# A plain first gate/up pair, modulation bursts placed anew at the feed-forward starts, and four bursts moved into the third layer's attention

## The chip, the cores and the metric

The kernel runs on one core of one Trainium2 chip. The metric is the device time of one execution in microseconds (us). Engines are named as in the profile: PE is TensorE (PEld its weight loads), DVE VectorE, ACT ScalarE, POOL GpSimd, and SP SyncE, which issues nearly all DMAs.

## The reference

One inference step of a four-layer diffusion transformer. 640 tokens (512 latent, 128 prompt) of 1024 features run through four layers, each with another attention: neighbourhood, sliding window, multi-head latent with low-rank queries and keys (MLA), and grouped queries. The latent and the prompt tokens have a modulation of their own in each layer, computed from the two conditioning vectors.

```python
def adaln(cond, w_mod, b_mod):
    m = jax.nn.silu(cond) @ w_mod + b_mod
    return [t[:, None, :] for t in jnp.split(m, 6, axis=-1)]

def modulate(h, shift, scale):
    return h * (1 + scale) + shift

def swiglu(h, w_gate, w_up, w_down):
    return (jax.nn.silu(h @ w_gate) * (h @ w_up)) @ w_down
...
    for li in range(DEPTH):
        mp = adaln(c_ctx[None, :], w_mod[li], b_mod[li])
        ms = adaln(c, w_mod[li], b_mod[li])
        hp = modulate(rms_norm(xp, norm1_g[li]), mp[0], mp[1])
        hs = modulate(rms_norm(xs, norm1_g[li]), ms[0], ms[1])
        ...
        xp = xp + mp[2] * op
        xs = xs + ms[2] * os_
        xp = xp + mp[5] * swiglu(modulate(rms_norm(xp, norm2_g[li]), mp[3], mp[4]), ffn_w_gate[li], ffn_w_up[li], ffn_w_down[li])
        xs = xs + ms[5] * swiglu(modulate(rms_norm(xs, norm2_g[li]), ms[3], ms[4]), ffn_w_gate[li], ffn_w_up[li], ffn_w_down[li])
```

`w_mod` is 1024 x 6144 per layer, the feed-forward's hidden width 2816.

## The kernel before, in words

Everything is float32. A product is made of three matmuls: each operand is split into a high and a low part (`hh`/`hl` for activations, `whi`/`wlo` for weights), and high x high, high x low and low x high are summed in a bank of PSUM. Features lie on the partitions in eight blocks of 128, tokens along the free axis in two halves of 320 (latent 0 to 319; latent 320 to 511 with the prompt), so that a matmul is 128 x 128 by 128 x 320. The split of a weight is one copy on ACT and one subtraction on DVE or POOL (`two`, L315).

**The feed-forward part** (`rest`, L798) first finishes the attention's output projection (`halves_first`, L580): the last two feature blocks are done first for one half of the tokens, then for the other. After each block, `stat` (L483) squares and sums the new features, and a matmul with a matrix of ones (tile `consts`) gives the sums over features; the reciprocal root of them scales the activations. `make_b` (L628) then makes the activations' high and low parts. Gate and up are computed in pairs of matrices of 256 hidden columns, 11 pairs a layer. Each matrix goes by the Strassen-Winograd scheme (`gate_up`, L707): weights and activations are cut into 2 x 2 quadrants, four sums of weights S1 to S4 (`make_a`, L684) and four combinations of activations T1 to T4 (`make_b`) replace the eighth product of quadrants, so that a matrix has seven blocks of 12 matmuls (`block`, L699) in place of eight. The quadrants "11" and "21" of the activations are the first half's, "12" and "22" the second's; "12" is used in combinations only. Block results are summed on DVE into the tiles `sv` and `y`. The down projection follows after 4, 4 and 3 pairs.

**The bursts.** The next layer's modulation is computed beside the feed-forward's matmuls. `mod_part` (L416) issues 16 small matmuls at a time (L424): the conditioning vectors against 4 tiles `rawm` of 512 KB, half of the rows of 1024 columns of `w_mod`. This group is called a burst here; the profile counts it as 32 rows. Two bursts make 1024 columns; their results are turned by two small matmuls (`modev`). `mod_load` (L448) issues the next four loads behind each burst; there are four buffers of `rawm`, so a load can start only when the burst before it has read them. `fill` (L468) issues one more burst, `rest` calls it twice behind the output projection (`EDGE`, L821), then in equal steps between the matrices, and twice at the end. The generator's first `fill` is the load alone.

**The order of the work.** Each engine runs its queue in order. The order is fixed when the program is built: a scheduler gives each instruction a place by its priority (the program's order, with `high_priority` and `issue_after` to move some) and by its own estimate of when operands are ready. PE, DVE and SP can thus run what the program writes later. Weights of 256 KB (`raw`) and the bursts' loads share SP's queue.

**The third layer's attention** (`Mla.body`, L1482) makes the first two heads' operands in `first_group` (L1639): queries of head group 0 are normalized on DVE, transposed on PE (`trs`, L1009), copied to `qn`; the rotary parts go through `pe2` and are transposed too; then the keys (`ktok`). `products_q(1)`, the 30 matmuls for the queries of the second head group, is written behind them, but before the change it ran ahead of the transposes. Then `units` computes scores, softmax and values. All bursts for the fourth layer's modulation are in the third's feed-forward part.

Of the kernel before, what the change touches and what calls it, by code (L numbers as in the profile page):

```python
# [14 lines left out]
P = 128  # L15
D = 1024
ND = 8
# [245 lines left out]
class Net:  # L263
# [6 lines left out]
    def mm(self, out, lhsT, rhs, start, stop):  # L270
        return self.nc.tensor.matmul(out, lhsT=lhsT, rhs=rhs, start=start, stop=stop, skip_group_check=True)  # L271

# [195 lines left out]
    def fill(self, n):  # L468

        for _ in range(n):  # L470
            while self.filler:
                try:
# [3 lines left out]
                    self.filler.pop(0)  # L476

    def flush(self):
        while self.filler:
            self.fill(1)  # L480
# [144 lines left out]
    def make_b(self, pool, L, B, raws):  # L625
# [36 lines left out]
        for i in range(HALF):  # L662
            for d in (i, i + HALF):
                raw(d, hi)
                p, m = raws[d][:, NL:], more[:, d:d + 1]
                nc.scalar.activation(p, p, AF.Identity, bias=m)
            a, b, t = raws[i], raws[i + HALF], t3[i // 2][:, i % 2]
            self.sub(nc.vector, t, b[:, hi], a[:, hi])
            self.sub(nc.vector, a[:, hi], a[:, hi], a[:, lo])
            two("T1", i, hi, a[:, hi])  # L670
# [7 lines left out]
        for i in range(HALF):  # L678
            two("T4", ND + HALF + i, lo, raws[i + HALF][:, lo])
        for i in range(HALF):  # L680
            two("22", i + HALF, hi, raws[i + HALF][:, hi], shift[:, i + HALF, 0:1])
        yield
# [15 lines left out]
    def block(self, out, A, B, start, stop):  # L698

        h, l = self.two(A, self.nc.vector)  # L700
        for k, (xh, xl) in enumerate(B):
            c = slice(k * P, (k + 1) * P)
            self.mm(out, h[:, c], xh, start and k == 0, False)
            self.mm(out, h[:, c], xl, False, False)
            self.mm(out, l[:, c], xh, False, stop and k == len(B) - 1)

    def gate_up(self, fp, L, name, i, B, pair):  # L707
# [31 lines left out]
        yield  # L739
        if i == 0:  # L740
            self.block(d, A["S1"], B["T1"], True, True)
        self.block(b, A["S2"], B["T2"], True, True)
        add(v1, b, s1)
        if i:
            self.block(d, A["S1"], B["T1"], True, True)
        self.block(b, A["S3"], B["T3"], False, True)
# [7 lines left out]
        if up:  # L754
            for r in (1, 0):
                hi, lo = (fp.tile([P, T], F32R, tag="a", name=n, bufs=16) for n in ("ah", "al"))
                nc.scalar.copy(hi, pair[r])
                self.sub(nc.vector, lo, pair[r], hi.bitcast(F32))
                pair[r] = (hi, lo)
        yield  # L760
# [38 lines left out]
    def rest(self, L):  # L799

        nc, tc, a = self.nc, self.tc, self.a
        with tc.tile_pool(name=f"ffn{L}", bufs=1, reuse_waits="tile") as fp:
            self.slots(fp)
            todo = 0
            if L + 1 < self.depth:
                c0 = self.mod_done.get(L + 1, 0)
                todo = (6144 - c0) // (4 * MODW) * (ND // BURST) + 1 - 2 * EDGE
                self.filler = [self.mod_parts(L + 1, c0, 6144, fp)]
            B, raws = {}, {}
            B_steps = self.make_b(fp, L, B, raws)  # L810
# [5 lines left out]
            def first_half(d):  # L816
                with tc.issue_after(self.last.ins):
                    next(B_steps)
            self.halves_first(lambda d: self.weights((L, "wo", d), 1), self.o_act[4:], L, 2, LAST,
                              after_wo, first_half)  # L820
            self.fill(EDGE)  # L821
            done = 0
# [4 lines left out]
            def ahead(m):  # L827
                n, i = mats[m]
                gens[m] = self.gate_up(fp, L, n, i, B, pairs[i])
                next(gens[m])  # L830
            ahead(0)
            ahead(1)
            next(gens[0])
            next(gens[1])
            next(B_steps)
            for part, (i0, i1) in enumerate(PAIRS):
                if part:
                    ahead(2 * i0)
                for m in range(2 * i0, 2 * i1):
                    if m > 1:  # L840
                        next(gens[m])
                    next(gens[m])
                    if 0 < m < 2 * i1 - 1:
                        ahead(m + 1)
                    next(gens[m])
                    while done < todo * (m + 1) // len(mats):
                        self.fill(1)
                        done += 1
# [16 lines left out]
class Attn:  # L865
# [142 lines left out]
    def tr(self, out, in_):  # L1008
        self.nc.tensor.transpose(out, in_, self.net.ident)  # L1009

# [468 lines left out]
class Mla(Full):  # L1479
# [4 lines left out]
    def body(self):  # L1484
# [9 lines left out]
        with net.tc.tile_pool(name="heads", bufs=1, reuse_waits="tile") as self.ap:  # L1494
            self.Q, self.ktok = {}, {}
            self.now(self.products_q(0), self.products_k(0))
            for g in range(4):
# [8 lines left out]
            self.job(net.out_part(2, 0), 16, 10, 16)  # L1506
            self.first_group()
            self.units()
            self.now(self.acts(8))
# [130 lines left out]
    def first_group(self):  # L1640
# [10 lines left out]
        for e in range(2):  # L1651
            x = self.tile([P, T], "qn", 3, F32R)
            self.stack(x, 64 * e, tl, net.col("mla_qn"))
            self.hd[e] = [x, None, None]
        pe = q[:, :, 256:]
        self.times(pe, ss[:, 1], 4, 32)
        self.rope(pe, 4, 16, self.qtab)

        pe2 = self.tile([P, NTT, P], "pe2")
        for e in range(2):  # L1660
# [7 lines left out]
        for e in range(2):  # L1668
            z = self.tile([P, T], "qpe", 2, F32R)
            self.stack(z, 64 * e, tl)  # L1670
            self.hd[e][2] = z
        tk = self.trs(k, slice(0, P), 6)
        for e in range(2):
# [4 lines left out]
            nc.scalar.copy(y[o, 1], y[r, 1].bitcast(F32))  # L1678
            self.hd[e][1] = y
        self.now(self.products_q(1))  # L1680
        for t in range(6):
            self.times(k[:, t:t + 1, P:], sk[:, t:t + 1, 2:], 2, 64, nc.gpsimd)
# [72 lines left out]
```

## Time and profile before

| | |
|---|---|
| runs, us | 3213.5, 3220.17, 3220.33 (median 3220.17) |
| profiled execution, us | 3216.05 (span 3214.0) |
| PE busy | 3029.7 us (94%), 21901 instructions |
| DVE, ACT, POOL busy | 67%, 48%, 19% |
| first FFN, from the end of attention to the second layer | about 378 to 881 us |
| third layer's attention | about 1635 to 1957 us |
| third FFN | about 1957 to 2461 us |

A busy PE is not yet a PE at its peak: matmuls overlap, and one is counted with its whole duration (313 ns for 128 x 320) although the next begins earlier. What a stretch is worth is read from the spacing of the matmuls' starts, and from the chain of waits, which follows the work that ended last back to the beginning.

### The profile page before, as it was taken

What the parts mean: (1) busy time and instruction counts of PE and PEld (TensorE: products, weight loads), DVE (VectorE), ACT (ScalarE), POOL (GpSimd) and SP (SyncE); (2) the same over time, 40 slices, a digit from 0 to 9 for tenths busy, and PEclk for the clock granted to TensorE, in tenths of its full rate; (3) what the DMA queues carried; (4) which work ended last, traced back from release to release, by engine and by line L of the source; (5) the groups of instructions that cost most, each with busy time, mean ns of one, the idle gap of its engine ahead of it and who ended that gap; (6) DMA issues with size and microseconds to landing.
All of it is one profiled execution on the core that took longest, in us unless ns stands there. A gap on an engine that the chain in (4) does not pass through costs nothing.

```text
span 3214.0 us, 57273 instructions
## 1 busy us (share of the span) xinstructions
PE 3029.7 (94%) x21901; PEld 2841.6 (88%) x21901; DVE 2161.6 (67%) x4522; ACT 1528.5 (48%) x3264; POOL 607.1 (19%) x691
## 2 busy tenths in 40 slices
PE   7998989999999989999986899899999999899999
PEld 6997879999988779999985778899998878799999
DVE  5555587666586768585768766867575775875765
ACT  4555454333356755242446664434243576543432
POOL 2553200000044420000025542000001553100000
PEclk9998999999999999999998999999999999899999
DMA  8346563232433342222211224522233111132322
GB/s 265 97 123 208 176 224 102 70 92 94 147 102 128 112 155 76 83 83 76 87 53 37 63 75 143 170 89 80 83 132 118 52 32 32 53 99 70 96 66 86
DMA packets 159027, 331.41 MB, mean 103 GB/s; under 512 B 18592, under 2 KB 40480, under 8 KB 158752
## 3 DMA queue, kind: packets, MB, share of 16 engines
q1 hardware_dynamic: 155584, 323.46, 32.3%
q8 instruction: 173, 2.83, 0.4%
q10 hardware_dynamic: 3168, 4.28, 0.4%
q14 instruction: 102, 0.84, 0.1%
HBM read 303.86 MB, written 4.28 MB: 96 GB/s over the span
## 4 chain that ended last, share of the span: by engine, by line
PE 81%; DVE 8%; DMA 5%; ACT 3%; issue 1%; POOL 1%; SPq 0%; DVEq 0%; ACTq 0%; POOLq 0%
PE big L271 53%; PE sm L271 18%; PE S L271 6%; PE tp L1009 3%; DMA rawm<-in_wmod 3%; DMA k<-k 1%; PE tp L271 1%; DMA raw<-in_wall 1%; DVE st L1030 1%; ACT p L1031 1%; DVE x L603 1%; DVE wlo L319 1%; ACT pt L285 0%; DVE qs L958 0%; DVE hl L999 0%
## 5 line engine op out<-in xcount | busy, mean ns | idle before, releaser
L271 PE MATMUL big<-hh,whi 128*128 128x320 f32 x2720 | 825.4, 313 | 11.7 <-ACT hh L645 5.6
L271 PE MATMUL big<-hl,whi 128*128 128x320 f32 x2720 | 829.0, 311 | 6.3 <-DVE hl L649 3.6
L271 PE MATMUL big<-hh,wlo 128*128 128x320 f32 x2720 | 821.0, 310 | 0.0
L318 ACT CAST whi<-raw 128x512 fp32r<-128x512 f32 (+2 forms) x636 | 383.3, 607 | 709.2 <-PE big L271 554.0
L271 PEld LDWEIGHTS big<-hh,whi 128*128 128x128 f32 x2720 | 508.8, 190 | 25.8 <-ACT hh L645 7.8
L271 PEld LDWEIGHTS big<-hl,whi 128*128 128x128 f32 x2720 | 510.1, 189 | 12.0 <-DVE hl L649 6.2
L271 PEld LDWEIGHTS big<-hh,wlo 128*128 128x128 f32 x2720 | 508.2, 189 | 0.1
L319 POOL TENSOR_TENSOR wlo<-raw,whi 128x512 fp32r<-128x512 f32 (+2 forms) x148 | 196.7, 1342 | 1634.0 <-ACT whi L318 1600.6
L319 DVE TENSOR_TENSOR wlo<-raw,whi 128x512 fp32r<-128x512 f32 (+1 forms) x488 | 325.1, 670 | 142.1 <-ACT whi L318 136.1
L318 ACT CAST whi<-sum 128x512 fp32r<-128x512 f32 x352 | 217.6, 619 | 300.1 <-PE big L271 264.6
L271 PE MATMUL big<-ah,wlo 128*128 128x320 f32 x1408 | 329.1, 309 | 0.0
L271 PE MATMUL big<-ah,whi 128*128 128x320 f32 x1408 | 329.0, 310 | 0.0
L271 PE MATMUL big<-al,whi 128*128 128x320 f32 x1408 | 328.6, 309 | 0.0
L319 DVE TENSOR_TENSOR wlo<-sum,whi 128x512 fp32r<-128x512 f32 x352 | 240.8, 684 | 54.5 <-ACT whi L318 52.9
L1041 POOL TENSOR_SCALAR p<-p,st 128x640 f32<-128x640 f32 (+2 forms) x256 | 197.7, 778 | 285.2 <-DVE st L1040 172.0
L603 DVE SCALAR_TENSOR_TENSOR x<-big,mod,x 128x128 f32<-128x128 f32 (+2 forms) x384 | 146.2, 432 | 150.7 <-PE big L271 150.3
L271 PEld LDWEIGHTS big<-ah,whi 128*128 128x128 f32 x1408 | 237.3, 188 | 1.3 <-issue 0.8
L271 PEld LDWEIGHTS big<-al,whi 128*128 128x128 f32 x1408 | 237.3, 188 | 0.3
L271 PEld LDWEIGHTS big<-ah,wlo 128*128 128x128 f32 x1408 | 237.3, 188 | 0.2
L271 PE MATMUL sm<-whi,hh 128*128 128x256 f32 (+1 forms) x770 | 225.1, 297 | 1.7 <-DVE qs L287 1.1
L271 PE MATMUL sm<-wlo,hh 128*128 128x256 f32 (+1 forms) x770 | 223.3, 292 | 0.2 <-POOL wlo L319 0.2
L271 PE MATMUL sm<-whi,hl 128*128 128x256 f32 (+1 forms) x770 | 223.1, 291 | 0.0
(260 smaller groups left out, 5419.3 us busy)
## 6 DMA issues: line engine op xcount, KB each, us to landing
raw<-in_wall SPq DMA_DIRECT2D x676, 256.0 KB, 2.6
rawm<-in_wmod SPq DMA_DIRECT2D x176, 512.0 KB, 5.8
k<-k SPq DMA_DIRECT2D x38, 384.0 KB, 4.2
bias<-in_nabias SPq DMA_DIRECT2D x16, 576.0 KB, 7.2
raw<-in_wmod SPq DMA_DIRECT2D x32, 256.0 KB, 5.7
qpe<-pes SPq DMA_DIRECT2D x56, 80.0 KB, 2.1
raw<-in_wall SPq DMA_DIRECT2D x32, 128.0 KB, 2.1
out_y<-x ACTq DMA_DIRECT2D x8, 320.0 KB, 2.2
```

Source lines behind the costliest of these rows:

```text
L271: return self.nc.tensor.matmul(out, lhsT=lhsT, rhs=rhs, start=start, stop=stop, skip_group_check=True)
L318: self.nc.scalar.copy(hi, raw)
L319: eng.tensor_tensor(lo, raw, hi.bitcast(F32), ALU.subtract)
L603: self.last = self.nc.vector.scalar_tensor_tensor(xs, halves[b][:, p0:p1], self.mcol(L, i, d, c), xs, ALU.mult, ALU.add)
L1009: self.nc.tensor.transpose(out, in_, self.net.ident)
L1030: nc.vector.tensor_reduce(nm, s, axis=AX.XY, op=ALU.max, negate=True)
L1031: nc.scalar.activation(p.rearrange("p (a b) -> p a b", a=2), s, AF.Exp, bias=nm, accum_out=den)
L1041: nc.gpsimd.tensor_scalar(p, p, rd, 1.0, ALU.mult, ALU.mult)
```

## The change

It has three parts.

1. *A plain first pair.* In each layer the first pair of gate and up is computed by `first_pair` instead of `gate_up`: no sums of weights, eight blocks a matrix in place of seven, four banks of PSUM side by side, and first the whole first half of the tokens (quadrants "11" and "21"), then the second ("12" and "22"). `make_b` makes "12" as an operand of its own (tile `h12`), and "12" and "22" ahead of the combinations T1 to T4. In `gate_up` the special order of the first pair falls away.
2. *Bursts at the feed-forward's beginning.* The first load is issued at the beginning of `rest`. The two bursts behind the output projection become one, tied to the last matmul issued (`fill_here`), and one follows between the first pair's halves. The rest are spread as before, with a count that is one smaller.
3. *Four bursts of the fourth layer in the third's attention.* `body` opens the bursts for the first 2048 of 6144 columns, and `first_group` places four of them: behind the query transposes, ahead of the first scores, and on either side of `products_q(1)`. The tile `pe2` takes the buffer tag `ropet`. The third feed-forward part has four bursts fewer.

```diff
     def mm(self, out, lhsT, rhs, start, stop):
-        return self.nc.tensor.matmul(out, lhsT=lhsT, rhs=rhs, start=start, stop=stop, skip_group_check=True)
+        self.last_mm = self.nc.tensor.matmul(out, lhsT=lhsT, rhs=rhs, start=start, stop=stop, skip_group_check=True)
+        return self.last_mm
...
+    def fill_here(self):
+
+        with self.tc.issue_after(self.last_mm.ins):
+            self.fill(1)
...
+            x12 = pool.tile([P, 2, 320], F32R, tag="a", name="h12", bufs=16)
+            slots.append([x12[:, j:j + 1].rearrange("p a b -> p (a b)") for j in range(2)])
+            two("12", len(slots) - 1, slice(0, 320), raws[i][:, hi], shift[:, i, 0:1])
+            two("22", i + HALF, hi, raws[i + HALF][:, hi], shift[:, i + HALF, 0:1])
+        yield
+        for i in range(HALF):
...
-        for i in range(HALF):
-            two("22", i + HALF, hi, raws[i + HALF][:, hi], shift[:, i + HALF, 0:1])
         yield
...
+    def first_pair(self, fp, L, B, pair):
+
+
+        nc = self.nc
+        W = {}
+        for name in ("gate", "up"):
+            for r, f in enumerate((0, NF // 2)):
+                for n in range(2):
+                    raw = self.slot("raw")
+                    nc.sync.dma_start(raw, self.a["wall"][WIDX[L, name, f][0] + n])
+                    W[name, r, n] = self.two(raw, nc.vector)
+        pair.extend(fp.tile([P, T], F32, tag="t", name="y", bufs=4) for _ in range(2))
+        for c in range(2):
+            for name in ("gate", "up"):
+                for r in range(2):
+                    out, y = self.ps("big")[:, :320], pair[r][:, 320 * c:320 * c + 320]
+                    for n in range(2):
+                        h, l = W[name, r, n]
+                        for k, (xh, xl) in enumerate(B[f"{n + 1}{c + 1}"]):
+                            w = slice(k * P, (k + 1) * P)
+                            self.mm(out, h[:, w], xh, n == 0 and k == 0, False)
+                            self.mm(out, h[:, w], xl, False, False)
+                            self.mm(out, l[:, w], xh, False, n == 1 and k == HALF - 1)
+                    if name == "gate":
+                        self.silu = nc.scalar.activation(y, out, AF.Silu)
+                    else:
+                        nc.vector.tensor_tensor(y, y, out, ALU.mult)
+            yield
+        self.pair_parts(fp, pair)
+        yield
...
         self.block(a, A["12"], B["21"], False, True)
         result(0, 0, a)
         yield
-        if i == 0:
-            self.block(d, A["S1"], B["T1"], True, True)
         self.block(b, A["S2"], B["T2"], True, True)
         add(v1, b, s1)
-        if i:
-            self.block(d, A["S1"], B["T1"], True, True)
+        self.block(d, A["S1"], B["T1"], True, True)
         self.block(b, A["S3"], B["T3"], False, True)
...
-                todo = (6144 - c0) // (4 * MODW) * (ND // BURST) + 1 - 2 * EDGE
+                todo = (6144 - c0) // (4 * MODW) * (ND // BURST) - 2 * EDGE
                 self.filler = [self.mod_parts(L + 1, c0, 6144, fp)]
+                self.fill(1)
...
-            self.fill(EDGE)
+            self.fill_here()
...
-            ahead(0)
-            ahead(1)
-            next(gens[0])
-            next(gens[1])
+            first = self.first_pair(fp, L, B, pairs[0])
+            next(first)
             next(B_steps)
+            self.fill_here()
+            next(first)
+            next(B_steps)
+            next(first)
...
             self.Q, self.ktok = {}, {}
+
+            net.filler = [net.mod_parts(3, 0, 2048, self.ap)]
+            net.fill(1)
             self.now(self.products_q(0), self.products_k(0))
...
             self.first_group()
+            assert len(net.mod_todo) == 0
+            net.flush()
...
+        net.fill_here()
         pe = q[:, :, 256:]
...
-        pe2 = self.tile([P, NTT, P], "pe2")
+        pe2 = self.tile([P, NTT, P], "ropet")
...
+        net.fill_here()
         tk = self.trs(k, slice(0, P), 6)
...
+        net.fill_here()
         self.now(self.products_q(1))
+        net.fill_here()
```

**In the order of PE, the beginning of the first layer's feed-forward part.** The last product of the output projection's first half is followed by the statistics (`t,consts`), then the second half. Before the change (`rawm,cond` is a burst):

```order
L271 MATMUL big<-hl,whi 128x320
L271 MATMUL big<-hh,wlo 128x320
L271 MATMUL sm<-rawm,cond 32x256 x16
L271 MATMUL big<-t,consts 128x320
L271 MATMUL big<-hh,whi 128x320
L271 MATMUL big<-hl,whi 128x320
L271 MATMUL big<-hh,wlo 128x320
```

After it:

```order
L271 MATMUL big<-hl,whi 128x320
L271 MATMUL big<-hh,wlo 128x320
L271 MATMUL big<-t,consts 128x320
L271 MATMUL big<-hh,whi 128x320
L271 MATMUL big<-hl,whi 128x320
L271 MATMUL big<-hh,wlo 128x320
L271 MATMUL big<-hh,whi 128x320
```

The burst no longer stands ahead of the first half's statistics; the second half's products follow these in both.

Some 30 instructions further on, behind the output projection's second half (`big_5091` before, `big_5099` after). Before the change, with the second burst, the second half's statistics, and then the first blocks of the two matrices in two banks (`big_5186`, `big_5224`):

```order
L271 MATMUL big_5091<-hh_4528,wlo_4987 128x320
L271 MATMUL sm_5145<-rawm_5168,cond_61 32x256 x4
L271 MATMUL sm_5145<-rawm_5166,cond_61 32x256 x4
L271 MATMUL sm_5145<-rawm_5164,cond_61 32x256 x4
L271 MATMUL sm_5145<-rawm_5162,cond_61 32x256 x4
L271 MATMUL big_5107<-t_4768,consts_78 128x320
L271 MATMUL big_5107<-t_5023,consts_78 128x320
L271 MATMUL big_5186<-hh_5053,whi_5192 128x320
L271 MATMUL big_5224<-hh_5053,whi_5228 128x320
L271 MATMUL sm_5742<-consts_78,modev_5740 128x8 x2
L271 MATMUL big_5186<-hl_5054,whi_5192 128x320
```

After it, the first burst stands behind the statistics, and four banks begin together:

```order
L271 MATMUL big_5115<-t_4776,consts_78 128x320
L271 MATMUL big_5115<-t_5031,consts_78 128x320
L271 MATMUL sm_5145<-rawm_4739,cond_61 32x256 x4
L271 MATMUL sm_5145<-rawm_4737,cond_61 32x256 x4
L271 MATMUL sm_5145<-rawm_4735,cond_61 32x256 x4
L271 MATMUL sm_5145<-rawm_4733,cond_61 32x256 x4
L271 MATMUL big_5220<-hh_5061,whi_5172 128x320
L271 MATMUL big_5246<-hh_5061,whi_5184 128x320
L271 MATMUL big_5272<-hh_5061,whi_5196 128x320
L271 MATMUL big_5298<-hh_5061,whi_5208 128x320
```

The next burst comes 96 products later, ahead of the first product with `h12`.

**PE in the beginning of the third layer's attention.** The last rows of products, then the transposes (`tp<-consts`) of queries, rotary parts, keys, and the first scores (`S`). Before (the products `sm` are the end of `products_q(1)`; `pe2` is printed as `pe`):

```order
L271 MATMUL sm<-whi,hh 128x384
L271 MATMUL sm<-wlo,hh 128x384
L271 MATMUL sm<-whi,hl 128x384
L1009 MATMUL tp<-consts,qs 128x128 x5
L1009 MATMUL tp<-consts,pe_19562 128x128 x5
L1009 MATMUL tp<-consts,ktok 128x128 x6
L1009 MATMUL tp<-consts,qs 128x128 x5
L271 MATMUL S<-k,qn 128x320 x3
L271 MATMUL S<-kpe,qpe 128x320
```

After it:

```order
L271 MATMUL S<-whi,hh 128x512
L271 MATMUL S<-wlo,hh 128x512
L271 MATMUL S<-whi,hl 128x512
L1055 MATMUL tp<-consts,qs 128x128 x5
L271 MATMUL sm<-rawm,cond 32x256 x16
L1055 MATMUL tp<-consts,ropet 128x128 x5
L1055 MATMUL tp<-consts,ktok 128x128 x6
L1055 MATMUL tp<-consts,qs 128x128 x5
L271 MATMUL sm<-rawm,cond 32x256 x16
L271 MATMUL S<-k,qn 128x320 x3
L271 MATMUL S<-kpe,qpe 128x320
L271 MATMUL S<-k,qn 128x320 x2
```

The products of the second group's queries went behind the first scores; two bursts came between the transposes.

**SP at the same place,** where it issues the third layer's weights (`raw`) and the spread of queries and keys for the next heads (`qpe`, `k`). Before:

```order
L308 DMA raw<-in_wall 128x384 x2
L308 DMA raw<-in_wall 128x512
L308 DMA raw<-in_wall 128x384 x2
L308 DMA raw<-in_wall 128x512 x2
L1691 DMA qpe<-pes 32x640 x8
L1006 DMA k<-k 64x1536 x2
L308 DMA raw<-in_wall 128x512
```

After it:

```order
L309 DMA raw<-in_wall 128x512
L456 DMA rawm<-in_wmod 128x1024 x4
L309 DMA raw<-in_wall 128x384 x2
L456 DMA rawm<-in_wmod 128x1024 x12
L1746 DMA qpe<-pes 32x640 x8
L1052 DMA k<-k 64x1536 x2
L309 DMA raw<-in_wall 128x512 x3
```

The loads of all four bursts stand ahead of the first spread.

## Rows read from the trace of the kernel before

**Rows 1.** The page, chain that ended last: shares of the span by line.

```profile
PE big L271 53%; PE sm L271 18%; PE S L271 6%; PE tp L1009 3%; DMA rawm<-in_wmod 3%; DMA k<-k 1%; PE tp L271 1%; DMA raw<-in_wall 1%; DVE st L1030 1%; ACT p L1031 1%; DVE x L603 1%; DVE wlo L319 1%; ACT pt L285 0%; DVE qs L958 0%; DVE hl L999 0%
```

**Rows 2.** The chain, its longest piece in the first FFN: start, us, what.

```profile
476.26 298.72 PE big L271 x2036
```

**Rows 3.** Windows, FFN starts: us; busy (instructions) PE, PEld, DVE, ACT, POOL; clock; DMA.

```profile
405.50:476.20 70.70, 59.64 (x502) 49.13 (x501) 60.61 (x134) 40.84 (x87) 4.12 (x4) 0.95 0.63 224
1174.30:1223.00 48.70, 37.72 (x289) 30.38 (x289) 40.24 (x94) 29.38 (x65) 1.45 (x2) 0.91 0.44 157
1982.30:2057.10 74.80, 61.26 (x502) 49.59 (x501) 60.82 (x134) 41.04 (x87) 4.12 (x4) 0.93 0.62 212
2754.60:2799.70 45.10, 30.42 (x142) 26.07 (x140) 38.90 (x89) 30.17 (x64) 3.21 (x3) 0.81 0.08 24
```

**Rows 4.** The same windows, instructions on the tile rawm (bursts) alone.

```profile
405.50:476.20 70.70, 15.91 (x224) 7.81 (x224) 0.95 0.63 224
1174.30:1223.00 48.70, 9.58 (x128) 4.54 (x128) 0.91 0.44 157
```

**Rows 5.** The same windows, instructions on the tile consts (statistics) alone.

```profile
405.50:476.20 70.70, 4.37 (x20) 2.99 (x20) 0.95 0.63 224
1174.30:1223.00 48.70, 3.86 (x16) 2.43 (x16) 0.91 0.44 157
2754.60:2799.70 45.10, 3.64 (x8) 1.47 (x8) 0.81 0.08 24
```

**Rows 6.** PE's timeline, first and fourth start: start, us, instruction, idle before.

```profile
405.58 1.94 PE L271 MATMUL sm<-rawm,cond 128*32 128x256 f32 x32
...
410.16 0.81 PE L271 MATMUL big<-t,consts 128*128 128x320 f32 x2 [2.65 <-DVE t L496]
...
2758.35 1.43 PE L271 MATMUL big<-t,consts 128*128 128x320 f32 x2 [3.58 <-DVE t L496]
```

**Rows 7.** The chain in the first FFN start, two loads of bursts.

```profile
417.03 7.89 DMA rawm<-in_wmod
...
428.42 6.49 DMA rawm<-in_wmod
```

**Rows 8.** PE's waits by what released them: us, times, longest.

```profile
PE sm L271 <- DMA rawm<-in_wmod: 27.4, 14, 4.3
```

**Rows 9.** Lines view, DVE, 413 to 453 us: count, busy us, mean ns.

```profile
L649 DVE SCALAR_TENSOR_TENSOR hl<-raw,mod,hh 128x320 fp32r<-128x320 f32 x16 | 8.6, 542 | 0.0
L656 DVE TENSOR_TENSOR raw<-raw,rstd 128x320 f32<-128x320 f32 x16 | 7.3, 482 | 0.0
L319 DVE TENSOR_TENSOR wlo<-sum,whi 128x512 fp32r<-128x512 f32 x6 | 4.1, 681 | 2.3 <-ACT whi L318 2.3
...
L719 DVE TENSOR_TENSOR sv<-big,sv 128x320 f32<-128x320 f32 x2 | 0.9, 475 | 0.0
```

**Rows 10.** PE's timeline, fourth start, the products behind the statistics.

```profile
2761.18 0.47 PE L271 MATMUL big<-hh,whi 128*128 128x320 f32 x1
2761.45 0.47 PE L271 MATMUL big<-hl,whi 128*128 128x320 f32 x1
...
2763.58 0.31 PE L271 MATMUL big<-hh,whi 128*128 128x320 f32 x1
2763.73 0.31 PE L271 MATMUL big<-hl,whi 128*128 128x320 f32 x1
```

**Rows 11.** Windows, beginning of the third layer's attention; columns as in group 3.

```profile
1695.00:1715.00 20.00, 8.49 (x28) 6.07 (x28) 19.13 (x39) 10.08 (x19) 7.54 (x11) 0.50 0.05 14
1715.00:1775.00 60.00, 50.94 (x343) 40.98 (x343) 40.43 (x86) 40.88 (x92) 29.98 (x42) 0.94 0.22 53
```

**Rows 12.** PE's timeline in that stretch: its longest wait.

```profile
1701.64 1.33 PE L1009 MATMUL tp<-consts,pe 128*128 128x128 f32 x5 [9.77 <-ACT pe L1661]
```

**Rows 13.** The chain in that stretch: products of the second group's queries.

```profile
1684.56 3.95 PE sm L271 x21
```

**Rows 14.** SP's own queue, waits by what released them.

```profile
SPq L455 <- PE sm L271: 162.1, 87, 13.1
```

More of the change, by code (lines that the diff above doesn't have):

```diff
@@ L705, in block, with pair_parts @@
             self.mm(out, l[:, c], xh, False, stop and k == len(B) - 1)
+    def first_pair(self, fp, L, B, pair):
[26 more added lines that the diff above has]
+        yield
+    def pair_parts(self, fp, pair):
+        for r in (1, 0):
+            hi, lo = (fp.tile([P, T], F32R, tag="a", name=n, bufs=16) for n in ("ah", "al"))
+            self.nc.scalar.copy(hi, pair[r])
+            self.sub(self.nc.vector, lo, pair[r], hi.bitcast(F32))
+            pair[r] = (hi, lo)
     def gate_up(self, fp, L, name, i, B, pair):
@@ L754, in gate_up @@
         if up:
[L755 to L759, printed above, removed]
+            self.pair_parts(fp, pair)
         yield
@@ L841, in rest @@
                         next(gens[m])
-                    next(gens[m])
+                        next(gens[m])
                     if 0 < m < 2 * i1 - 1:
                         ahead(m + 1)
-                    next(gens[m])
+                    if m > 1:
+                        next(gens[m])
                     while done < todo * (m + 1) // len(mats):
@@ L1008, in tr @@
     def tr(self, out, in_):
-        self.nc.tensor.transpose(out, in_, self.net.ident)
+        self.net.last_mm = self.nc.tensor.transpose(out, in_, self.net.ident)
     def trs(self, x, c, n):
```

## The prediction, on record before the result

> **What bounds the kernel now.** I read the chain of waits first, then the four stretches in which a feed-forward part (FFN) begins, then the beginning of the third layer's attention. The chain [rows 1] lies on TensorE (PE), and its largest piece is the FFN matmuls. Inside an FFN it is one unbroken run: 2036 matmuls in 298.72 us [rows 2], 0.1467 us each. There only a change in the number of PE instructions counts. The FFN starts are another matter. The windows view [rows 3] has the four stretches from the last output-projection matmul until PE runs freely: 70.7, 48.7, 74.8 and 45.1 us. Take the instructions out: 502 in the first, of which 224 belong to bursts [rows 4] and 20 to statistics [rows 5], leave 258 product matmuls; the second has 289 - 128 - 16 = 145; the third has the first one's 502 again; the fourth, without bursts, 142 - 8 = 134. The profile counts a burst as 32 rows and 1.94 us [rows 6], so 224 rows are 7 bursts and 128 are 4. Products at 0.1467 us, bursts at 1.94, and the statistics at half of their busy time (a matmul's busy time is about twice its spacing) make 37.8 + 13.6 + 2.2 = 53.6 us of work in the first, 21.3 + 7.8 + 1.9 = 31.0 in the second, 53.6 in the third, 19.7 + 1.8 = 21.5 in the fourth. **Lost are 17.1, 17.7, 21.2 and 23.6 us, together 79.6.**
>
> The losses have two causes. Where bursts stand close together each waits for its own weights: a load takes 6.49 to 7.89 us in the chain [rows 7], and the next one is issued only when the burst before it has read the buffers. PE's waits for it sum to 27.4 us, in 14 places [rows 8]. The other cause is VectorE (DVE). At the fourth start there are no bursts, and DVE works 38.90 of the 45.10 us while PE's products need 21.5 [rows 3]: it makes the activations and their combinations, sums weights and splits them. Before this comes the wait for the statistics of the first half, 2.65 us behind the burst at the first start, 3.58 without one at the fourth [rows 6].
>
> **The change part by part.** *Plain first pair.* The seven blocks of two matrices, 168 matmuls, become 192: 24 more per layer, 96 in all, at 0.1467 us = **+14.1 us**, all on PE's path. It relieves DVE: per layer 6 splits at 0.681 us, 8 weight sums of the same size, which I count alike, and 10 result additions at 0.475 go, and 4 operations at 0.542 come, for the new operand [rows 9]: 4.1 + 5.4 + 4.8 - 2.2 = 12.1 us less. ScalarE loses six splits and two evictions and gains four operations; it is not the bound there (30.17 of 45.10 us [rows 3]). Above all the order of need changes. The first 96 matmuls need only the first half's activations, four banks in step: an activation of 0.482 + 0.542 us on DVE [rows 9] serves 12 matmuls, 1.76 us. Before, the same activation served 6, 0.88 us, and the third block already needed the combinations.
>
> *Bursts at the starts.* Only one now stands between the statistics and the pair, and one between the pair's two halves; the rest lie among later matrices, with much more than a load's 7.9 us between them. So the 27.4 us of waits for burst weights should mostly go. What stays, the two waits at the ends of the first and third FFN, is part of what else I count as unchanged. In exchange the wait for the first half's statistics stands empty: where the burst covered 1.94 us, PE now idles 2.65 + 1.94 = 4.6 us.
>
> What stays lost has no row; I bound it. From below: 5 us per start, about the empty wait of 4.6 us. From above: 14 per start, somewhat under the 17 us that the first start lost with its waits for weights. For the first and third start I take 10: 4.6 for the empty wait, some 1.6 for the second half's statistics, which the second burst no longer covers, some 2.3 for a slow clock behind the gap (the fourth start has it already: products 0.267 us apart, 0.120 more than usual, on some 19 of them [rows 10]), and 1.5 for the pair itself. For the second I take 5, since it has fewer bursts to move, and for the fourth 10, since 12.1 us of DVE work leave a stretch in which DVE was late by the whole loss. That is 35 of the 79.6: **-44.5 us**, nearer to the lower bound (20) than to the upper (56), as both causes named above are taken away at once.
>
> Behind the gap the row shows PE at the lower level of its clock [rows 10], and the mean granted clock at the fourth start is 0.81 against 0.95 at the first [rows 3]. By the Trainium skill, TensorE: Matmul & The Clock Gate, section "Why this matters for your kernels", PE should not stand idle between matmul bursts, as its clock then falls to half; this speaks against taking the burst out of the wait. The trace agrees at the fourth start, and what a longer slow stretch would make of the sum is a rival below.
>
> *Bursts in the third layer's attention.* Four bursts leave the third FFN: 4 x 1.94 = **-7.8 us** of unbroken PE work. They come into a stretch in which DVE is the bound: in 20 us DVE is busy for 19.13 and PE for 8.49, and PE waits 9.77 us in one piece [rows 11, 12]. Two bursts fall into this idle time and cost nothing if it stays. The other two, and 30 matmuls of the second head group's queries, which before stood ahead of the wait (21 of them are 3.95 us [rows 13], so 5.6 for 30), come 3.9 + 5.6 = 9.5 us later, into 60 us in which PE is idle for 60 - 50.94 = 9.1 us [rows 11]. Against this, DVE no longer has the second group's copies and sums of squares in the full stretch, so the long wait can shrink. From below I bound the gain by 6 us, some two thirds of the 9.77; from above the loss by 8 us, nearly all of the work that is added late. I take **+1 us**, as PE's free time there is just used up.
>
> *Queues.* SyncE (SP) issues in order, and a burst's load waits for the burst before it: 87 such waits make 162.1 us already [rows 14]. A moved load holds up what is queued behind it: in the FFN the 256 KB weight loads, in the third layer the spread of the queries' rotary part and of the keys for the next heads. In the order, the weight matrix behind a held load is first used some 100 matmuls (15 us) after the burst that frees it, against a load's 6.5 to 7.9 [rows 7]. From below it costs nothing; from above one load's 6 us at two places. I take **+2 us**.
>
> Sum: 14.1 - 44.5 - 7.8 + 1 + 2 = -35.2 us. The profiled execution took 3216.05 us, so 3180.9; it lies 4.1 us under the median of the runs, 3220.17, so a median of **3185 us**. What a measurement can tell from no change is 0.2%, 6.4 us.
>
> **The rivals.** (a) DVE still ends the starts: only the waits for burst weights go, and the emptied statistics waits take 8 of the 27.4 us back. Then 14.1 - 19.4 - 7.8 + 3 = -10.1, **3210 us**. For it: at the fourth start DVE is busy 86% of the time. Against: 12.1 us of its work go, and the need is spread over 28 us instead of 25. Chance 0.11.
> (b) The starts lose only the empty wait, 20 in all, nothing queues, and the third layer's attention gains 5: 14.1 - 59.6 - 7.8 - 5 = -58.3, **3162 us**. Chance 0.06.
> (c) Slower: SP. Some ten bursts now stand among matrices that load their weights through the same queue (five in the first FFN, two in the second, three in the third). If a weight load behind a held burst load comes late each time, PE stops. Without the 2 us for queues I have -37.2, so stalls of 3.7 us at ten places give back everything, and 4.4 us make it slower by more than 0.2%. At 6.5 us each, the shortest load of [rows 7], it is +28, **3248 us**. Against it stand the 15 us of lead in the order; for it, that SP's order is fixed and [rows 14] shows a wait of 13.1 us. By the Trainium skill, DMA: Bandwidth & Descriptors, section "Anatomy of one DMA — SWDGE (gpsimd) path", a semaphore wait is served on the issuing sequencer before dispatch; the SPq wait in the profile agrees, and it is why later loads stand behind it. Chance 0.07.
> (d) The clock: after the emptied wait the four-bank phase runs at the lower level throughout, since DVE feeds it with short gaps. 96 matmuls x 0.120 = 11.5 us per layer, 9.2 more than I counted, 37 in all: **3222 us**, no change. The clock rule cited above would have it so. Against it: at the fourth start PE is back at 0.147 us within 6 us, though DVE feeds it no better [rows 10]. Chance 0.04.
> That the change doesn't do what it says I leave out: the order shows each move.
>
> **How the numbers follow.** The forecast has 0.72, with a range of its own of 3166 to 3204: 20 to 55 us lost, the attention's -6 to +8, SP's 0 to 12, not all at one end. The range for 8 in 10 reaches up to (a): 3164 to 3210. Faster by over 0.2% (under 3213.8): 0.71 of the forecast, 0.07 of (a), 0.06 of (b), 0.84. Within 0.2%: 0.08, most of it (a) and (d). Slower (over 3226.6): 0.08, from (c) and a bad (d).
>
> **What would show it.** In the changed profile: waits of PE for burst weights under 12 us instead of 27.4; at each start an empty wait for statistics of 4 to 5 us, followed by products 0.267 us apart for a few us; the pair's 192 matmuls in 29 to 33 us; DVE under 85% busy in that stretch; in the third layer's attention the wait of 9.77 us cut by bursts, and the first half of the heads ending within 8 us of where it did, relative to its start. I am wrong if PE waits in the middle of the FFNs for raw weights, if the pair's first half waits for DVE at each activation, or if the attention grows by over 8 us.

## The result and the profile after

The changed kernel takes **3159.32 us** (median of 4 runs, 3157.35 to 3164.3), the kernel before 3216.84 us on the same chip (3213.0 to 3220.33): a ratio of 0.9824, interval 0.9805 to 0.9843. It is 57.5 us faster. Forecast were 3185 us and a range of 3164 to 3210; the direction was right and the gain too small by 40%. The profiled execution took 3159.6 us, with a span of 3157.8.

The four starts, as windows from the last product of the projection's first half to the end of the first pair (columns as in [rows 3]):

```profile
406.30:449.70 43.40, 40.19 (x292) 36.57 (x291) 37.77 (x89) 31.50 (x69) 2.12 (x2) 0.96 0.38 128
1163.90:1205.00 41.10, 38.78 (x293) 35.27 (x292) 37.02 (x88) 31.36 (x69) 0.90 (x1) 1.00 0.39 135
1962.00:2002.90 40.90, 38.76 (x293) 35.29 (x292) 36.69 (x87) 30.90 (x68) 0.79 (x2) 1.00 0.40 135
2713.00:2750.10 37.10, 34.72 (x226) 33.02 (x225) 33.17 (x77) 29.22 (x65) 0.00 (x0) 1.00 0.13 37
```

Each holds 24 products of the projection and the pair's 192: 216 x 0.1467 = 31.7 us. With two bursts (3.9) and the statistics (1.2) that is 36.8 us of work in the first three and 32.9 in the fourth. Lost are 6.6, 4.3, 4.1 and 4.2 us, 19.2 in all, where [rows 3] gave 79.6 and I had expected 35 to stay. The granted clock is 1.00, the upper level (2.4 GHz), in three of them. DVE is still busy 87 to 90% of the time, and PE's work now fills 85 to 90% of it: the two are nearly even.

The chain runs through the pair with one short break, 0.34 us in the second half (start, us, what; third layer). The first half's products stand 14.27/96 = 0.1486 us apart, beside [rows 2]'s 0.1467:

```profile
1972.37 14.27 PE big L271 x96
1986.64 1.86 PE sm L271 x32
1988.50 3.42 PE big L271 x22
1992.26 21.51 PE big L271 x146
```

PE's waits (us, times, longest) for burst weights are almost gone [rows 8]; none of the three that are left stands at an FFN's start. Those for the statistics have shrunk too, from 8.9 us:

```profile
PE big L271 <- DVE t L502: 5.7, 4, 2.1
...
PE sm L271 <- DMA rawm<-in_wmod: 3.6, 3, 2.6
```

The wait for the statistics that I put at 4.6 us is 2.11 us at the first start and 1.04 at the third. Only at the first does a slow clock follow: the granted clock is 0.57 in the four us behind the wait, and 1.00 behind the other three. PE's timeline (compare [rows 6, 10]):

```profile
408.61 1.02 PE L271 MATMUL big<-t,consts 128*128 128x320 f32 x2 [2.11 <-DVE t L502]
...
410.23 0.47 PE L271 MATMUL big<-hh,whi 128*128 128x320 f32 x1
410.49 0.47 PE L271 MATMUL big<-hl,whi 128*128 128x320 f32 x1
...
412.56 0.32 PE L271 MATMUL big<-hh,whi 128*128 128x320 f32 x1
412.71 0.31 PE L271 MATMUL big<-hl,whi 128*128 128x320 f32 x1
...
1963.19 0.81 PE L271 MATMUL big<-t,consts 128*128 128x320 f32 x2 [1.04 <-DVE t L502]
```

In the third layer's attention the longest wait [rows 12] is gone; the longest that is left stands ahead of the query transposes:

```profile
1669.65 1.30 PE L1055 MATMUL tp<-consts,qs 128*128 128x128 f32 x5 [5.87 <-DVE qs L1004]
```

SP's waits for bursts [rows 14] fell, and PE's list of waits has none for a weight load (`raw` from `in_wall`):

```profile
SPq L456 <- PE sm L271: 136.3, 79, 11.9
```

### The profile page after: what moved, and what is told of

Its sections match the earlier page's. It is cut to its first block, busy times and chain, and to the rows that moved or that the text cites. A ratio compares the mean times of both kernels' runs of the same rounds, so it can differ in the third digit from the quotient of the medians.

```text
span 3157.8 us, 57354 instructions
## 1 busy us (share of the span) xinstructions
PE 3021.5 (96%) x21997; PEld 2844.8 (90%) x21997; DVE 2112.1 (67%) x4442; ACT 1518.0 (48%) x3248; POOL 612.7 (19%) x691
## 5 line engine op out<-in xcount | busy, mean ns | idle before, releaser
L271 PE MATMUL big<-hl,whi 128*128 128x320 f32 x2688 | 814.9, 309 | 1.8 <-DVE hl L1045 1.8
L271 PE MATMUL big<-hh,whi 128*128 128x320 f32 x2688 | 811.1, 310 | 1.6 <-ACT whi L319 1.1
L271 PE MATMUL big<-hh,wlo 128*128 128x320 f32 x2688 | 808.5, 310 | 0.0
L320 POOL TENSOR_TENSOR wlo<-raw,whi 128x512 fp32r<-128x512 f32 (+2 forms) x148 | 206.9, 1413 | 1583.0 <-ACT whi L319 1550.4
L271 PEld LDWEIGHTS big<-hh,whi 128*128 128x128 f32 x2688 | 499.2, 188 | 10.3 <-issue 3.2
L271 PEld LDWEIGHTS big<-hl,whi 128*128 128x128 f32 x2688 | 501.4, 188 | 3.5 <-DVE hl L1045 2.8
L271 PEld LDWEIGHTS big<-hh,wlo 128*128 128x128 f32 x2688 | 499.4, 188 | 0.3
L319 ACT CAST whi<-sum 128x512 fp32r<-128x512 f32 x320 | 197.3, 620 | 278.6 <-PE big L271 240.7
L320 DVE TENSOR_TENSOR wlo<-sum,whi 128x512 fp32r<-128x512 f32 x320 | 218.5, 685 | 45.3 <-ACT whi L319 43.2
```

The source lines that it names most:

```text
L271: self.last_mm = self.nc.tensor.matmul(out, lhsT=lhsT, rhs=rhs, start=start, stop=stop, skip_group_check=True)
L319: self.nc.scalar.copy(hi, raw)
L320: eng.tensor_tensor(lo, raw, hi.bitcast(F32), ALU.subtract)
```

## The experiments

After the result there were two readings. **A:** DVE bounds the starts, and what the pair takes off it is what counts; the waits for burst weights lay over the same time. **B:** the two causes add up, as the prediction had it. Medians stand against the kernel before, measured beside each (3216.8 to 3218.4 us). The table has the length of each FFN in the profiled executions: from the end of the last product ahead of the first statistics (a product counted with its spacing) to the first statistics at the part's end (in the fourth layer, to PE's last instruction), read from PE's timeline.

| kernel | median, us | ratio, interval | FFN 1 | 2 | 3 | 4 |
|---|---|---|---|---|---|---|
| before | 3216.84 | | 466.3 | 452.4 | 470.4 | 455.4 |
| change | 3159.32 | 0.9824 (0.9805 to 0.9843) | 459.7 | 441.7 | 448.0 | 440.8 |
| e1 pair alone | 3174.09 | 0.9863 (0.9843 to 0.9883) | 462.9 | 441.4 | 461.5 | 440.9 |
| e2 bursts alone | 3213.75 | 0.9991 (0.9978 to 1.0005) | 468.1 | 453.9 | 466.8 | 456.4 |
| e3 no attention bursts | 3165.64 | 0.9843 (0.9826 to 0.9860) | 459.9 | 441.7 | 457.1 | 440.8 |
| e4 attention bursts alone | 3207.90 | 0.9975 (0.9961 to 0.9989) | 469.7 | 450.7 | 461.3 | 455.2 |
| e5 first burst early | 3160.74 | 0.9815 (0.9798 to 0.9831) | 456.6 | 440.4 | 447.0 | 440.7 |
| e6 old load on DVE | 3216.43 | 0.9989 (0.9980 to 0.9998) | 472.6 | 454.1 | 460.9 | 455.2 |
| e7 one end burst | 3167.37 | 0.9843 (0.9830 to 0.9857) | 460.2 | 441.7 | 450.0 | 440.7 |
| e8 late 22 | 3162.45 | 0.9824 (0.9811 to 0.9837) | 459.9 | 441.2 | 448.1 | 438.6 |
| e9 load inside the pair | 3197.17 | 0.9934 (0.9919 to 0.9949) | 464.6 | 448.1 | 456.0 | 451.0 |
| e10 early burst, sums held | 3166.31 | 0.9841 (0.9824 to 0.9858) | 460.1 | 441.6 | 449.9 | 440.7 |
| e11 change again | 3160.23 | 0.9824 (0.9807 to 0.9841) | 460.2 | 441.7 | 448.0 | 440.7 |
| e12 two attention bursts | 3173.51 | 0.9861 (0.9843 to 0.9879) | 459.7 | 441.7 | 454.2 | 440.8 |

**The parts alone.** e1 keeps `first_pair` and takes the other two parts out:

```diff
-                self.fill(1)
...
-            self.fill_here()
+            self.fill(EDGE)
...
             next(B_steps)
-            self.fill_here()
             next(first)
```

> The plain first pair alone, with the bursts called for as before (two behind the output projection, none moved into the third layer's attention). Theory A: the pair is what frees the starts, since VectorE no longer has to make sums, splits and combinations before PE can go on; the fourth layer, which has no bursts, falls by the 14 to 15 us that it falls in the full change, and the first three by nearly as much, less one wait of 2 to 4 us each between their two first bursts: in all 36 to 44 us under the kernel before. Rival B: the waits for burst weights (27.4 us) are a part of their own that the pair does not touch; then the first three starts gain little and the whole is 18 to 25 us under the kernel before.

e2 has the bursts of the change around the old first pair:

```diff
+                self.fill(1)
...
-            self.fill(EDGE)
+            self.fill_here()
...
             next(gens[1])
+            self.fill_here()
             next(B_steps)
```

> The bursts placed as in the change (load at the beginning, one behind the statistics, one inside the first pair), but the first pair by seven blocks as before, and no bursts in the third layer's attention. Theory A: the starts are then bound by VectorE, as the fourth start without any burst was (24.7 us lost); the waits for burst weights go and the same time is lost waiting for activations: between 8 us under and 6 us over the kernel before, and the fourth start unchanged. Rival B: the waits for burst weights are added on top of the rest: about 20 us under.

Both come out as A said. The pair alone brings 43.5 us of the 57.5; the bursts alone bring 0.1%, with 1 inside the interval. e1 alone wouldn't tell the readings apart, since in it the waits for burst weights fall too, to 9.0 us; its fourth FFN, which has no bursts, does: 14.5 us shorter. In e2 the waits for burst weights fall from 27.4 us [rows 8] to 7.5, and 12.1 us of this come back in two waits under DVE's and ACT's names. PE's waits of e2:

```profile
PE big L271 <- DVE t L502: 14.7, 4, 4.6
PE big L271 <- ACT hh L651: 11.9, 4, 4.4
...
PE sm L271 <- DMA rawm<-in_wmod: 7.5, 6, 3.1
```

(Before, `t` had 8.9 and `hh` 5.6 us.) Its longest wait for the statistics is 4.6 us: the price that I gave the emptied wait was right for the old pair at the first start (3.0 and 2.6 us at the second and third). With the plain pair it is not paid: in e2's first layer DVE has a split and a sum to do between the last product's end and the statistics, in the changed kernel it has neither.

**Bursts in the attention.** e3 is the change without its third part, e4 the kernel before with the third part alone.

> The full change without its third part: the fourth layer's four first bursts go back into the third feed-forward part. Theory A: these bursts cost their own 1.9 us each there and were nearly free in the attention: 6 to 10 us over the changed kernel (3165 to 3170 us). Rival C: the attention grew by what the bursts cost, so that nothing was won: within 3 us of the changed kernel.

> The kernel before with the third part alone: four bursts in the third layer's attention. Theory A: the third feed-forward part loses 7.8 us of PE work and the attention grows by 0 to 2: 5 to 12 us under the kernel before, the upper end if the burst waits at the third start also become fewer. Rival C: within 3 us of the kernel before.

Both come out as A said: 6.3 us over the change, 9.7 under the kernel before. The intervals of e3 and the change overlap, so the first of the two rests on the stretch: the third FFN is 9 us longer with the bursts (457.1 against 448.0, 470.4 against 461.3).

e1 and e3 differ in the bursts' places at the starts alone, and e3 is 8.4 us faster (the intervals overlap), with the first FFN 3.0 and the third 4.4 us shorter. So behind the plain pair the new places do bring something, where e2 had 3.9 us, not to be told from nothing. Reading B has this much for it: what the waits for bursts cost showed once DVE was relieved.

e12 leaves the first two in the attention:

```diff
-            net.filler = [net.mod_parts(3, 0, 2048, self.ap)]
+            net.filler = [net.mod_parts(3, 0, 1024, self.ap)]
...
-        net.fill_here()
         self.now(self.products_q(1))
-        net.fill_here()
```

> The full change with only the first two bursts in the third layer's attention, those between the transposes and ahead of the first scores; the other two go back into the third feed-forward part (+3.9 us there). If the third and fourth burst cost their 1.9 us each in the attention too: within 3 us of the repetition beside it. If they were hidden: 3 to 5 us over it. If they cost more than that there: up to 5 us under it.

The third FFN is 6.2 us longer than in e11, a little more than two bursts; the time is 13 us over e11, more than any of the three cases gave. Of the other 7 us in the profiles, 5.5 lie in the second layer's attention, which the edit doesn't touch, and 2.1 in the third's, which it does. So two bursts fewer did not make that attention shorter; that they were hidden there fits this, but isn't shown.

**What of the pair pays?** e6 gives DVE the old amount of work back, as sums and additions whose results nobody reads:

```diff
+        def load(n):
+            for j in range(n):
+                nc.vector.tensor_tensor(self.slot("sum"), raws[-1], raws[-2], ALU.add)
...
+        load(14)
...
+                    for j in range(2 if c == r == 0 else 1):
+                        nc.vector.tensor_tensor(self.slot("sum")[:, :320], out, self.x[:, 0, :320], ALU.add)
```

> The full change, with the work that the plain pair took off VectorE given back as idle work in the first pair of each layer: 14 sums of 128x512 ahead of the pair (8 sums and 6 splits were dropped) and 10 additions on its results. Theory D: the relief of VectorE by 12 us per layer is what pays; then the starts lose 8 to 12 us more each, and the time is 30 to 48 us over the changed kernel. Theory E: the order of need is what pays (an activation now feeds 12 matmuls, and no combination is needed before the third matrix), and VectorE has room for the old work; then 0 to 12 us over it, most of it in the waits for the statistics.

e8 makes the quadrant "22" behind the combinations again:

```diff
-            two("22", i + HALF, hi, raws[i + HALF][:, hi], shift[:, i + HALF, 0:1])
         yield
...
             two("T4", ND + HALF + i, lo, raws[i + HALF][:, lo])
+        for i in range(HALF):
+            two("22", i + HALF, hi, raws[i + HALF][:, hi], shift[:, i + HALF, 0:1])
```

> The full change with the activations' quadrant 22 made behind the combinations T1 to T4, as before the change, though the plain pair needs it in its second half. VectorE's work is the same, only its order is the old one. Theory E: 32 operations of about half a us, 16 us, now stand ahead of what PE needs next; PE waits 5 to 10 us per layer, 20 to 40 us over the changed kernel. Theory D: the order matters little, 0 to 8 us over it.

D holds, beyond the upper end of what was expected. The added work of e6 in its lines view (instructions, busy us, mean ns):

```profile
L725 DVE TENSOR_TENSOR sum<-raw 128x512 f32<-128x512 f32 x56 | 37.6, 704 | 1.2 <-DMA raw<-in_wall 1.1
...
L747 DVE TENSOR_TENSOR sum<-big,x 128x320 f32<-128x320 f32 x40 | 18.3, 481 | 0.4
```

37.6 + 18.3 = 55.9 us of work cost 57.1 us of time, 52.6 of them in the four FFNs: nearly a microsecond for a microsecond, and the whole gain is gone. DVE is busy for 2161.6 us in the kernel before, 2112.1 in the changed one and 2158.6 in e6. The fourth layer shows it best, as it has no bursts: 55.9/4 = 14.0 us of work make its FFN 14.4 us longer, as long as before the change. (In the first three, e6's built order also has the bursts closer together, and the waits for their weights rise from 3.6 to 11.7 us.) The ten additions read the pair's banks of PSUM, but no wait of PE names them. E falls with this run, as e6 keeps the new order of need. Half of the cost (33.9 - 5.7 = 28.2 us) is in the waits for the statistics, more than the kernel before had there (8.9 us), as all sums stand ahead of them here:

```profile
PE big L271 <- DVE t L502: 33.9, 4, 10.0
```

e8 doesn't test what it was meant to. The program writes "22" last, but the scheduler put it back: in the order built, each of its four `hl` stands behind one of "12" (`h`), and all four ahead of the first addition for T2 (L683), as in the changed kernel (there at 425.12, 426.39 and 437.36 us). (T2's low parts have the same name, but need that addition first.) DVE's timeline of e8, first layer; the other three are alike:

```profile
424.63 0.54 DVE L655 SCALAR_TENSOR_TENSOR h<-raw,mod,h 128x320 fp32r<-128x320 f32 x1
...
425.90 0.55 DVE L655 SCALAR_TENSOR_TENSOR hl<-raw,mod,hh 128x320 fp32r<-128x320 f32 x1
...
435.42 0.89 DVE L683 TENSOR_TENSOR raw<-raw 128x320 f32<-128x320 f32 x2
```

So its 3162.45 us say nothing of a late "22". Neither the order of need, nor the four banks, nor an activation that feeds 12 matmuls instead of 6 was tried by itself.

e9 puts work into the pair alone, three additions on each bank's result and none ahead of the statistics:

```diff
+                    for j in range(3):
+                        nc.vector.tensor_tensor(self.slot("sum")[:, :320], out, self.x[:, 0, :320], ALU.add)
```

> The full change with 24 idle additions of 0.475 us (11.4 us per layer) on VectorE inside the plain pair, three on each bank's result, and none ahead of the statistics. In e6 the old work stood ahead of the statistics, and the waits for these grew most. If VectorE is the bound inside the pair too (37.0 of 41.1 us busy at the second layer's pair), PE waits for what does not fit, about 7 us per layer: 20 to 30 us over the changed kernel. If only the place ahead of the statistics matters: 0 to 8 us over it.

```profile
L741 DVE TENSOR_TENSOR sum<-big,x 128x320 f32<-128x320 f32 x96 | 43.1, 498 | 0.0
```

43.1 us of work cost 37 us against e11, more than the 20 to 30 expected. The four FFNs are 4.4, 6.4, 8.0 and 10.3 us longer, 29 in all; the other 8 us of the 37 lie outside of them. The fourth layer is again the cleanest: 10.8 us of work, 10.3 us longer. The pair itself runs through there (192 products in 28.89 us of the chain), and PE waits in one piece, ahead of the third matrix (its timeline):

```profile
2790.69 0.64 PE L271 MATMUL big<-hh,whi 128*128 128x320 f32 x1 [11.05 <-ACT whi L319]
```

The split that it waits for belongs to the next weights, which queue behind the added work. In the first three layers the wait behind the pair has the name of burst weights, 4.8, 4.7 and 5.8 us, as the built order has 12 products between two bursts there where the change has 72:

```profile
PE sm L271 <- DMA rawm<-in_wmod: 20.9, 7, 5.8
```

So only the fourth layer separates the two causes. A load early in the stretch thus shows as a wait for statistics, one inside it as a wait for the third matrix: DVE's work is one queue through the whole start.

**Smaller waits.** e5 has the first burst ahead of the statistics again (`fill(1)` in place of `fill_here()`); e10 does this too, and ties the third matrix's weight sums behind the last residual addition; e7 has one burst less at the end of an FFN:

```diff
-                todo = (6144 - c0) // (4 * MODW) * (ND // BURST) - 2 * EDGE
+                todo = (6144 - c0) // (4 * MODW) * (ND // BURST) - EDGE - 1
```

> The full change with the first burst of each feed-forward part back ahead of the first half's statistics, where the kernel before had it. The changed kernel's trace has an empty wait of 2.3, 1.4 and 1.2 us there in the first three layers, and products at half pace behind it in the first layer. If the empty wait costs what it shows, and the burst fills it: 3 to 8 us under the changed kernel (3151 to 3156 us). If the burst only pushes the statistics back: within 3 us of it.

> The full change with the first burst ahead of the statistics (as in the run with the first burst early) and the third matrix's weight sums tied behind the last residual addition, so that no sum stands ahead of the statistics on VectorE. If the 0.6 to 1.9 us of sums between the residual additions are what is left of the waits for the statistics, these shrink to under 1 us, and the time is 4 to 12 us under the changed kernel's repetition beside it. If the sums then come late for the third matrix: 0 to 8 us over.

> The full change with one burst in place of two at the ends of the first and third feed-forward parts (one more among the matrices). The changed kernel's chain has a load of 6.67 us between the two at the end of the third. If that load is on the path: 4 to 11 us under the changed kernel (two ends, less what the second burst covered there). If the next layer's first activations are late anyway: within 3 us of it.

> The changed kernel once more, unedited, for a comparison on the same chip: within 8 us of 3159.3 us. It also shows how far the first layer's attention, which no edit touches, varies between executions (405 to 412 us so far).

e11 repeats the change and agrees within 1 us. In e5 the four FFNs are 5.5 us shorter in all than in the change, most of it in the first (456.6 against 459.7 us), where the slow clock had followed the wait; the medians (3160.74 and 3159.32) don't show it. In e10 the waits for the statistics are gone (0.2 us left), but the median is 6 us over e11's, the second of the two cases expected; the four FFNs are 7.6 us longer than in e5, which has the same early burst and doesn't hold the sums. In e7 the first and third FFN are 0.5 and 2.0 us longer for the added burst, and the next layers' first products come 1.1 and 1.4 us sooner behind the statistics at the parts' ends, so that nothing is won where the edit acts: in e7's chain the place of the load of 6.67 us is taken by products and by the next layer's first activations. The median is 8 us over the change's, not 4 to 11 under it; the intervals overlap, and of the 12.8 us between the two profiles 5.7 lie in the first layer's attention, which no edit touches. No kernel tried beats the changed one clearly.

## Why the prediction was off

*The pair's cost and relief.* The step that failed is "what stays lost", put at 35 us and -44.5 for the change; 19.2 stay, about -60. I counted 96 matmuls as +14.1 us "all on PE's path" and took the losses down by separate pieces. The runs show one bound in the main: at the starts DVE set the length, so the matmuls filled time in which PE had waited, and the stretch shrank by about what left DVE. That was in the text, 12.1 us per layer, but only as a support. Taken as the sum it gives -48 us for the four starts; e1 measured -43.5, e6 +57 for 55.9 us put back. The fourth layer, without bursts, shows it by itself: 455.4 to 440.8, 14.6 us shorter with 24 matmuls more, and 455.2 with the load put back. I had left 10 us lost there and 10 at the first and third start; 4.2, 6.6 and 4.1 are. The first layer gained least, 6.6 us (3.4 in e1); why is not shown. Of the signs named, DVE under 85% busy did not come.

*The order of need* was said to matter "above all". What it brings stays open: e8 left the order as it was, and e6 keeps the new order and loses the whole gain.

*The waits for burst weights*, 27.4 us, were to go, and went (3.6 left). But e2 shows that their going alone brings next to nothing, and e1 that the pair leaves 9.0 us of them without moving a call: the third burst there stands behind the pair's 192 matmuls. Their going is worth some 8 us only together with the pair (e1 to e3).

*The emptied wait* of 4.6 us and the slow clock behind it, 2.3 at the first and third start, were too high: 1.0 to 2.1 us, and a slow clock at the first start alone, where products stand 0.267 us apart and are back at 0.15 four us later. By the Trainium skill, TensorE: Matmul & The Clock Gate, "Why this matters for your kernels", PE should not stand idle for long between matmul bursts, as its clock then falls to half. The first start agrees that it falls; how long an idle wait does it, these traces don't tell, as at the first start of the kernel before PE idled 2.65 us [rows 6] and the granted clock stayed at 1.00. The rival (d) didn't occur: 0.1486 us in the pair.

*The attention's bursts*: -7.8 and +1 were near the mark. The third FFN gave 9 us in both comparisons. The attention, from the second FFN's last statistics to the last product ahead of the third FFN's first, measures 345.5 to 351.5 us in nine profiles with four bursts (the middle one 349.4), and 343.3 to 347.8 in four without any (middle 346.8).

*Queues*: +2, and no wait of PE for a weight load was seen; rival (c) did not occur. Rival (a), 3210 us, is the very mechanism that e6 measures, but I had let it stand beside the relief instead of letting the relief decide it. Rival (b), 3162 us, had the size of the starts right (20 us lost, 19.2 measured), with a chance of 0.06. That was luck in part: it let the empty wait alone be lost, which is 1.0 to 2.1 us of the 4 to 7 at a start, and its 5 us gain in the attention is not seen.

## What to carry to other kernels

Where a stretch has waits under several names, look first for the engine that is busy through nearly all of it (here DVE, 86%), and price a change by what it takes off that engine: 12.1 us per layer, 48 in all, was near the 43.5 us that the pair brought, with 24 more matmuls a layer on the waiting engine. A wait for a transfer that lies over the same time brings little when it goes alone; it returns in part under the next name. To test which engine bounds a stretch, give it idle work of a known length and see whether the time grows by as much, best in a stretch without the other suspect (here the fourth layer). Where a scheduler places the instructions, look in the built order whether an edit moved what it was meant to: in e8 it did not.

## What was not expected of the hardware

The spread between executions of one kernel was larger than the first three runs told: 3209.6 to 3224.1 us in 21 executions of the kernel before. The first layer's attention, which no edit touches, took 405.4 to 412.0 us in the profiles, so differences under some 8 us between two profiles were read here by stretches only. How long PE had idled did not tell whether a slow clock followed: a wait of 2.11 us was followed by products 0.267 us apart, those of 1.0 to 1.3 us were not, and neither were the 2.65 us at the first start before and the 2.56 us at e2's third.
